# A hybrid decoder block on one core: the sums for the down weights paced two at a time, and a warm-up of fp32r products in seven operand orders

## The chip, the core and the metric

The kernel runs on one core of a Trainium2 chip. The metric is the device time of one execution in microseconds. The profile of one execution, taken on the chip, gives a span from the first to the last instruction.

Five engines work side by side, each through its own queue of instructions in order: TensorE (PE, with its weight loads PEld), VectorE (DVE), ScalarE (ACT), GpSimd (POOL) and SyncE (SP). In this kernel SyncE issues nearly all loads and stores, and GpSimd issues the transfers that add in DRAM.

## The reference

```
h = rms_norm(x, g_mix_pre);  z = h @ w_in                      # x: 512 x 1024
y_pool = pool_mixer(z[:, :512]) @ w_pool_out
y_rnn  = rg_lru_branch(z[:, 512:1536], z[:, 1536:2560]) @ w_rg_out
x = x + rms_norm((gate_pool * y_pool + gate_rnn * y_rnn) @ w_o, g_mix_post)

h = rms_norm(x, g_ffn_pre);  up = h @ w_up                     # 1024 x 6144
hid = gelu(causal_dwconv(up[:, :3072])) * up[:, 3072:]
x = x + rms_norm(hid @ w_down, g_ffn_post)                     # 3072 x 1024

ple = rms_norm(p @ w_ple_proj, g_ple_post)
x = x + sigmoid(rms_norm(x, g_ple_gate) @ w_ple_gate) * ple
```

All inputs are fp32. `w_in` has 4608 columns: 512 for the pooling, 1024 and 1024 for the recurrence, and 2048 for the two gates.

## The kernel before

**Arithmetic.** Every fp32 operand is split into two fp32r parts, a rounded `hi` (a copy on ACT, L193 or L412) and the rest `lo` (a subtraction on VectorE, L189 or L414). A product of two operands is three products of parts, the helper `mm3` (L196 to L200): hi x hi, hi x lo, lo x hi. L198, L199 and L200 therefore stand for nearly all of TensorE's work. The order of TensorE's instructions is the order of the program (`manual_schedule`, L116). The other engines' order is set by a planner from the program order, with priorities (`urgent()`, `high_priority`) and some orders written out by hand (`behind`).

**The opening.** The columns `col` are loaded and `ones` is set (L208). A warm-up follows on TensorE: ten fp32 products of `ones` with itself, 128 columns each (L214 to L216); a product of fp32 shows in the profile as two instructions. Then the transposed input arrives in eight tiles, ACT scales each to `hi` and VectorE makes `lo` (L466, L467), and the first four tiles of the recurrence's input are computed together: 8 chunks x 3 parts x 4 tiles of 512 columns (L497 to L503). Behind them come the remaining tiles of `w_in`, in `in_tile`, with the first L198.

**The middle.** The recurrence, the pooling, their output products and `w_o`. The products with `w_o`, the up weights (for pairs 1 and later) and the down weights use a scheme of seven products for a 2 x 2 block (Strassen's, in the form with sums that follow from each other), so sums of weight blocks are needed: blocks 1, 2, 3 are plain and 5, 7, 6, 4 are sums, numbered by f.

**The up stage.** Pairs p = 0 to 11 of 128-wide column tiles of the gate half and of the linear half. From pair 1 on, `seven(p)` gives the order of a pair's products: f = 1, then 3 of the pair before, then 6, 2, 7, 5, 4. Each f is 24 products of 256 columns (`up_product`, L972). For the block sums of pairs 3 to 11 the four plain blocks are loaded by SyncE (L342, `raw`) and added on VectorE (L348); each is split by L193 and L189. ACT copies or negates results between banks at f = 1 (L985), f = 6 (L990), f = 7 (L992, L993) and f = 5 (L988, into `q5`). The two convolution steps on VectorE are L1000, and the products of `hidden` are L1009 and L1016. Weights are prepared four products ahead (`AHEAD`), six `raw` buffers in turn.

**The sums for the down weights.** `sums_of("wd")` (L253) yields 48 transfers of 512 KB: for each of f = 5, 7, 6, 4 six copies and then six additions in DRAM (`accum_op`) into `wsum`. For 6 and 4 the copies read a sum made before (in the profile `wdsum<-wdsum`); all others read `w_down`. `sum_in_dram` (L269) issues the next n on GpSimd's queue; the first of them waits for an instruction named by `after`, and each follows the one before in the queue. L1088 and L1089 call it once in a pair, after f = 5 from pair 2 on, for six transfers that wait for the copy at L988:

```
if f == 5 and p >= SUMS_FROM:
    sum_in_dram(down_sums, SUMS_EACH, q5_done[0])
```

The last of the 48 go out in pair 9. The down products (`down_product`, L1136) read the sums after the up stage.

**Buffers.** `quad("C")` takes the next of four C buffers, `slot()` the next of 25 m buffers, `bank()` the next of eight PSUM banks. A tile waits until the earlier owner of its buffer is no longer read.

Of the kernel before, what the change touches and what calls it, by code (L numbers as in the profile page):

```python
# [9 lines left out]
F32 = mybir.dt.float32  # L10
F32R = mybir.dt.float32r
AF = mybir.ActivationFunctionType
ALU = mybir.AluOpType

P = 128
S = 512
# [15 lines left out]
HALF = S // 2  # L32
# [14 lines left out]

UP_SUMS = (1, 2)

SUMS_FROM, SUMS_EACH = 2, 6  # L50


PLACES, PLACE_UP, PLACE_H2 = 64, 48, (1072, 46)
URGENT = 700
WARM = 10

FIRST = (0, 256), (256, 512), (512, 1024)
IN_ORDER = [("gate", _g) for _g in range(4)]
# [23 lines left out]
def block_kernel(  # L82
# [21 lines left out]
    ACT, V, PE = nc.scalar, nc.vector, nc.tensor  # L104
# [13 lines left out]
    def urgent():  # L118
        return tc.high_priority(offset=URGENT)
# [3 lines left out]
    def nm(s):  # L123
        uid[0] += 1
        return f"{s}{uid[0]}"

    def bank():
        return psum.tile([P, S], F32, tag="ps", name=nm("ps"))

    def temp(dt=F32, n=S):  # L130
        return tmp.tile([P, n], dt, tag="t", name=nm("t"))

    def slot(dt=F32):
        return mid.tile([P, S], dt, tag="m", name=nm("m"))

    def quad(tag, dt=F32R, place=0):
        t = big.tile([P, 4 * S + PLACES], dt, tag=tag, name=nm(tag))
        return t[:, place : place + 4 * S].rearrange("p (a c) -> p a c", a=4)
# [13 lines left out]
    def behind(ins, name):  # L152
        tc.add_manual_dep(
            ins.ins,
            name,
            mybir.DependencyInfo(mybir.DependencyClass.NoSync, mybir.DependencyReason.DATA),
            reason="order on the engine",
        )
# [24 lines left out]
        last_func[0] = ins.ins.name  # L183
        return ins

    last_copy, h2_done, z_done, q5_done = [None], [None], [None], [None]

    def sub(o, a, b):
        V.tensor_tensor(o, a, b, ALU.subtract)  # L189
# [17 lines left out]
    ones = slot()[:, :P]  # L207
# [4 lines left out]
    ACT.copy(warm, ones[:, 0:1])  # L212

    wps = bank()  # L214
    for _ in range(WARM):
        PE.matmul(wps[:, :P], ones, ones, start=True, stop=True)  # L216

    def c1(j):
        return col[:, j : j + 1]
# [33 lines left out]
    def sums_of(name):  # L253

        if name == "up":
            for p in UP_SUMS:
                for f, start, more in ((5, 11, 12), (7, 12, 22), (6, 5, 22), (4, 6, 21)):
                    yield usum[p, f], usum[p, start] if start < 10 else up_block(p, start), {}
                    yield usum[p, f], up_block(p, more), {"accum_op": ALU.add}
            return  # L260
        for f, start, more in ((5, 1, 0), (7, 0, 3), (6, 5, 3), (4, 6, 2)):
            for q in range(pieces[name]):
                yield wsum[name, f][q], piece_of(name, start, q), {}
            for q in range(pieces[name]):
                yield wsum[name, f][q], block_of(name, more, q), {"accum_op": ALU.add}
# [3 lines left out]
    def sum_in_dram(sums, n, after=None):  # L269

        for o, i, kw in islice(sums, n):
            ins = nc.gpsimd.dma_start(o, i, **kw)
            if after is not None:
                kind = mybir.DependencyClass.Sync, mybir.DependencyReason.DATA
                tc.add_manual_dep(ins.ins, after, mybir.DependencyInfo(*kind), reason="pace of the sums")
                after = None
            if last_sum[0] is not None:
                behind(ins, last_sum[0])
            last_sum[0] = ins.ins.name

    def seven(p):

        return [(p - (f == 3), f) for f in (SEVEN if p > 1 else SEVEN_1) if (f == 3 or p < NPAIR) and (f != 3 or p > 1)]
# [133 lines left out]
    def weight(key, ahead=AHEAD):  # L417
        i = order.index(key)
        while nxt[0] <= min(i + ahead, len(order) - 1):
            prep(order[nxt[0]])  # L420
            nxt[0] += 1
        return ready[key]
# [36 lines left out]
    for k in range(KD):  # L459
# [8 lines left out]
        if k % 2 == 1 and k < 7:  # L468
            if k > 1:
                xt = quad("C", F32)  # L470
                a = k // 2 - 1
# [25 lines left out]
    for k in range(KD):  # L497
        w = weight(("rx", k // 2), ahead=3)
        (wh, wl), (hh, hl) = w, ht(k)
        for i, (a, b) in enumerate(((wh, hh), (wl, hh), (wh, hl))):  # L500
            for m in range(4):
                o = (k % 2) * S + m * P
# [19 lines left out]
    mabs, e, f, s, s2, ncol, n2col = sp  # L522
# [293 lines left out]
    for m in range(KD):  # L816
        w = weight(("wpo", m))
# [3 lines left out]
        w = weight(("wrg", m))  # L821
# [7 lines left out]
        a, b = gate[m], gate[8 + m]  # L829
# [60 lines left out]
    hid, gb, ub = {}, {}, {}  # L890
# [5 lines left out]
    def products(o, w, i, form, start):  # L896
        for k in range(4):
            lhs = tuple(v[:, i, k * P : (k + 1) * P] for v in w)
            rhs = tuple(v[:, k, :] for v in form)
            mm3(o, lhs, rhs, start and k == 0, k == 3, skip_group_check=True)  # L900
# [69 lines left out]
    q5, act_g = {}, {}  # L970

    def up_product(f, p):  # L972
        for i in range(2):
            w = weight(("up", p, f))
            if f == 1 and p > 1:
                gb[i] = bank()
                if p == 2 and i == 0:
                    PE.matmul(gb[i], w[0][:, 0, :P], w[0][:, 0, :], start=True, stop=True)
            o = {1: zb, 6: zb, 7: zb, 2: gb, 4: gb, 3: ub, 5: {0: db, 1: db}}[f][i]
            a = HALF if f == 4 or (f, i) == (5, 1) else 0  # L980
            products(o[:, a : a + HALF], w, i, forms[f], f in (1, 5))
            z = zb[i][:, :HALF]
            with urgent():
                if f == 1 and p > 1:
                    ACT.copy(gb[i][:, :HALF], z)  # L985
                elif (f, i) == (5, 1):
                    q5[p] = temp()
                    q5_done[0] = ACT.copy(q5[p], o).ins.name  # L988
                elif f == 6:
                    ACT.activation(ub[i][:, :HALF], z, AF.Identity, scale=-1.0)  # L990
                elif f == 7:
                    ACT.copy(gb[i][:, HALF:], z)  # L992
                    z_done[0] = ACT.activation(ub[i][:, HALF:], z, AF.Identity, scale=-1.0).ins.name  # L993

    def gated_half(j, pg):
        a = temp()
        with urgent():
            ACT.activation(a, pg, AF.Identity, scale=c1(C_FW + 2 * NJ + j), bias=c1(C_FB + j))
            for d in (1, 2):
                V.scalar_tensor_tensor(  # L1000
                    a[:, d:], pg[:, : S - d], c1(C_FW + (2 - d) * NJ + j), a[:, d:], ALU.mult, ALU.add
                )
        act(a, a, AF.Gelu_apprx_tanh)
        act_g[j] = a

    def hidden(j, pu, q):
        hid[j] = hslot(j)
        if q is not None:
            V.tensor_tensor(  # L1009
                hid[j].rearrange("p (b c) -> p b c", b=2),  # L1010
                pu.rearrange("p (b c) -> p b c", b=2),
                q[:, None, :].to_broadcast([P, 2, HALF]),
                ALU.add,
            )
            pu = hid[j]
        V.tensor_tensor(hid[j], act_g[j], pu, ALU.mult)  # L1016
# [10 lines left out]
    for kind, n in O_AFTER:  # L1027
        if kind == "tr":
            h2_tile(n)
        elif kind == "up":  # L1030
            up_plain(n, 0)
        else:
            up_product(n, 1)
# [48 lines left out]
    down_sums = sums_of("wd")  # L1082
    for p in range(1, NPAIR + 1):
        for q, f in seven(p):
            if (q, f) == (1, 1):
                continue
            up_product(f, q)
            if f == 5 and p >= SUMS_FROM:  # L1088
                sum_in_dram(down_sums, SUMS_EACH, q5_done[0])  # L1089
            if f == 4:  # L1090
                for i in range(2):
                    gated_half(2 * q + i, gb[i])
            if f == 3:
                for i in range(2):
                    hidden(2 * q + i, ub[i], q5[q][:, i * HALF : (i + 1) * HALF])
# [97 lines left out]
    q5 = wpool.tile([P, 2, S], F32, tag="sum", name=nm("sum"), bufs=1)  # L1193
# [38 lines left out]
    for h in range(2):  # L1232
        for t in range(NT):
            i = 2 * (t % 2) + h
            o = temp()
# [3 lines left out]
            for a, b in parts:  # L1239
                ps = bank()  # L1240
                for k in range(KD):
                    if (h, t, k) == (0, 1, 3):
                        x3_tile(2)
                    w = weight(("wpg", k // 2, h))
# [86 lines left out]
```

## Time and profile before

| | us |
|---|---|
| median of 3 runs | 737.29 |
| lowest and highest | 736.93 and 737.32 |
| span of the profiled execution | 735.6 |
| TensorE busy in the span | 728.2 |
| VectorE, ACT, GpSimd busy | 577.8, 443.6, 82.7 |

The profiled execution's own time isn't given beside its span; the runs are 1.7 us longer in the median than the span.

In a timeline row stand start, duration (both in us from the start of the span), engine, line, operation, output<-inputs by the program's names, shape and count; a bracket holds the idle time of the engine before it and what ended it. A "q" behind an engine marks its queue. In the chain of work that ended last, each row is one step: start, us, what. A row of the view by windows holds the window and its length, then for each of PE, PEld, DVE, ACT and POOL the busy time with the number of instructions that touch the window, then the granted TensorE clock, the DMA share and GB/s. TensorE's ends are modelled: products overlap, so the pace is read from starts, and a busy TensorE needn't be at full pace.

### The profile page before, as it was taken

How to read it: one execution, taken by the hardware profiler on the slowest of the kernel's cores; microseconds unless marked ns; L12 is line 12 of the kernel's file. 1: busy time of each engine (PE TensorE's matmuls, PEld its weight loads, DVE VectorE, ACT ScalarE, POOL GpSimd, SP SyncE). 2: the span in 40 equal slices, each digit the busy share in tenths (PEclk: the TensorE clock that was granted, in tenths of full speed). 3: DMA queues.
4: the chain of work that ended last, by engine and by line, in shares of the span. 5: the costliest groups of instructions: out<-in, count | busy, mean ns of one | idle time of the engine just before them, and what ended most of it. 6: DMA issues, size and time to landing. Idle time of an engine off the chain costs nothing.

```text
span 735.6 us, 11212 instructions
## 1 busy us (share of the span) xinstructions
PE 728.2 (99%) x4281; PEld 641.8 (87%) x4281; DVE 577.8 (79%) x749; ACT 443.6 (60%) x670; POOL 82.7 (11%) x107
## 2 busy tenths in 40 slices
PE   9999999999999999999999999999999999999997
PEld 7887778888888888889999999999999888888886
DVE  4896735999646577776989999979799997788852
ACT  6746779844543334477856666666577756565721
POOL 0312112100000000120002323131210000001100
PEclk9999999999999999999999999999999999999999
DMA  8999786664788997895457798979798675768011
GB/s 328 382 309 268 166 238 175 154 198 131 267 297 267 325 327 286 306 333 180 144 191 267 176 321 234 315 206 273 253 246 297 206 250 193 266 201 270 18 58 57
DMA packets 64933, 172.53 MB, mean 235 GB/s; under 512 B 5808, under 2 KB 6448, under 8 KB 64560
## 3 DMA queue, kind: packets, MB, share of 16 engines
q1 hardware_dynamic: 50336, 129.78, 50.9%
q0 software_dynamic: 14400, 41.95, 24.1%
q8 instruction: 33, 0.54, 0.3%
q14 instruction: 20, 0.16, 0.1%
q10 hardware_dynamic: 144, 0.10, 0.0%
HBM read 155.03 MB, written 58.72 MB: 291 GB/s over the span
## 4 chain that ended last, share of the span: by engine, by line
PE 87%; DMA 7%; DVE 3%; issue 1%; ACT 1%; SPq 0%; POOL 0%; DVEq 0%; ACTq 0%
PE ps L198 28%; PE ps L199 28%; PE ps L200 28%; DMA raw<-in_w_up_dram 5%; DMA C<-in_x_dram 1%; DVE lo L189 1%; PE ps L858 1%; DVE raw L348 1%; PE ps L606 1%; DMA m<-in_x_t_dram 1%; PE ps L503 1%; DVE t L1000 1%; ACT C L486 0%; ACT hi L193 0%; SPq L403 0%
## 5 line engine op out<-in xcount | busy, mean ns | idle before, releaser
L189 DVE TENSOR_TENSOR lo<-raw,hi 128x1024 fp32r<-128x1024 f32 (+2 forms) x193 | 224.5, 1183 | 50.1 <-ACT hi L412 29.4
L198 PE MATMUL ps<-A,hi 128*128 128x256 f32 (+1 forms) x608 | 197.8, 325 | 1.1 <-ACT ps L985 1.1
L199 PE MATMUL ps<-A,hi 128*128 128x256 f32 (+1 forms) x608 | 197.1, 324 | 0.0
L200 PE MATMUL ps<-A,lo 128*128 128x256 f32 (+1 forms) x608 | 197.0, 324 | 0.0
L412 ACT CAST hi<-raw 128x1024 fp32r<-128x1024 f32 (+1 forms) x112 | 113.2, 1015 | 108.1 <-PE ps L199 43.2
L198 PEld LDWEIGHTS ps<-A,hi 128*128 128x128 f32 x608 | 114.3, 188 | 12.8 <-ACT ps L985 1.5
L200 PEld LDWEIGHTS ps<-A,lo 128*128 128x128 f32 x608 | 114.1, 188 | 10.1
L199 PEld LDWEIGHTS ps<-A,hi 128*128 128x128 f32 x608 | 114.1, 188 | 9.7
L198 PE MATMUL ps<-C,hi 128*128 128x256 f32 (+1 forms) x392 | 116.9, 298 | 0.0
L200 PE MATMUL ps<-C,lo 128*128 128x256 f32 (+1 forms) x392 | 116.6, 297 | 0.0
L199 PE MATMUL ps<-C,hi 128*128 128x256 f32 (+1 forms) x392 | 116.5, 297 | 0.0
L193 ACT CAST hi<-raw 128x1024 fp32r<-128x1024 f32 x78 | 80.6, 1052 | 33.2 <-PE ps L199 23.3
L198 PE MATMUL ps<-hi,A 128*128 128x512 f32 x224 | 87.4, 390 | 0.0
L200 PE MATMUL ps<-hi,A 128*128 128x512 f32 x224 | 87.2, 389 | 0.0
L199 PE MATMUL ps<-lo,A 128*128 128x512 f32 x224 | 87.1, 389 | 0.0
L198 PEld LDWEIGHTS ps<-C,hi 128*128 128x128 f32 x392 | 73.8, 188 | 2.8 <-ACT rb L441 0.2
L199 PEld LDWEIGHTS ps<-C,hi 128*128 128x128 f32 x392 | 73.8, 188 | 2.6
L200 PEld LDWEIGHTS ps<-C,lo 128*128 128x128 f32 x392 | 73.7, 188 | 2.5
L434 POOL TENSOR_TENSOR s<-s,mhalf 128x1 f32<-128x1 f32 (+1 forms) x21 | 15.8, 754 | 353.9 <-DVE s L447 334.6
L200 PEld LDWEIGHTS ps<-hi,A 128*128 128x128 f32 x224 | 42.0, 188 | 8.8
L199 PEld LDWEIGHTS ps<-lo,A 128*128 128x128 f32 x224 | 42.1, 188 | 8.6
L198 PEld LDWEIGHTS ps<-hi,A 128*128 128x128 f32 x224 | 42.0, 188 | 8.5
(191 smaller groups left out, 1026.2 us busy)
## 6 DMA issues: line engine op xcount, KB each, us to landing
raw<-in_w_up_dram SPq DMA_DIRECT2D x46, 512.0 KB, 7.4
wdsum<-in_w_down_dram POOLq DMA_DIRECT2D x36, 512.0 KB, 13.0
raw<-in_w_in_dram SPq DMA_DIRECT2D x32, 512.0 KB, 6.6
raw<-wdsum SPq DMA_DIRECT2D x24, 512.0 KB, 4.4
raw<-in_w_down_dram SPq DMA_DIRECT2D x18, 512.0 KB, 4.6
wosum<-in_w_o_dram POOLq DMA_DIRECT2D x12, 512.0 KB, 9.8
wdsum<-wdsum POOLq DMA_DIRECT2D x12, 512.0 KB, 12.0
parts<-hi SPq DMA_DIRECT2D x10, 512.0 KB, 3.9
```

The costliest lines, as they stand in the source:

```text
L189: V.tensor_tensor(o, a, b, ALU.subtract)
L193: last_copy[0] = ACT.copy(hi, src)
L198: PE.matmul(o, ah, bh, start=start, stop=False, **kw)
L199: PE.matmul(o, ah, bl, start=False, stop=False, **kw)
L200: PE.matmul(o, al, bh, start=False, stop=stop, **kw)
L348: V.tensor_tensor(o, a, b, ALU.add)
L412: ACT.copy(hi, raw)
L434: last_pow[0] = nc.gpsimd.tensor_tensor(y, v, mhalf[:, :n], ALU.pow).ins.name
L503: PE.matmul(rx[m], a[:, o : o + P], b, start=k == 0 and i == 0, stop=k == KD - 1 and i == 2)
L606: PE.matmul(ps, bd[pr, a, o], b[pr], start=i == 0, stop=i == 2)
L858: PE.transpose(ps[:, q * P : (q + 1) * P], a[:, q * P : (q + 1) * P], ident)
L1000: V.scalar_tensor_tensor(a[:, d:], pg[:, : S - d], c1(C_FW + (2 - d) * NJ + j), a[:, d:], ALU.mult, ALU.add)
```

## The change

The warm-up: VectorE clears 1024 columns of a C buffer, copies 512 of them into two m buffers as fp32r and copies the 1024 onto themselves as fp32r. TensorE then runs 14 products of fp32r with 512 columns, instead of 10 of fp32 with 128: each of seven orders of the moving operand, with both m buffers as the stationary one. The orders are plain; one column repeated; two columns 512 apart in turn; every second column; 16 columns of every 32; plain from column 1; plain from column 8. All values are zero.

The sums: two transfers are issued after each of the products f = 1, 6 and 5 of a pair, from pair 2 on, and wait for ACT's last copy there (L985, L990, L988). That is again six a pair.

```
-SUMS_FROM, SUMS_EACH = 2, 6
+SUMS_FROM, SUMS_AFTER, SUMS_EACH = 2, (1, 6, 5), 2
...
-WARM = 10
...
     wps = bank()
-    for _ in range(WARM):
-        PE.matmul(wps[:, :P], ones, ones, start=True, stop=True)
+    wq = quad("C")
+    V.memset(wq[:, 0:2, :].bitcast(F32), 0.0)
+    wv = wq[:, 0:2, :].rearrange("p a c -> p (a c)")
+    ws = [slot(F32R), slot(F32R)]
+    for w in ws:
+        V.tensor_copy(w, wv[:, :S].bitcast(F32))
+    V.tensor_copy(wv, wv.bitcast(F32))
+    moving = (
+        wv[:, 0:S],
+        wv[:, 0:1].to_broadcast([P, S]),
+        wv.rearrange("p (a b) -> p b a", a=2)[:, 0:HALF, :],
+        wv[:, 0 : 2 * S : 2],
+        wv.rearrange("p (c e) -> p c e", e=32)[:, :, 0:16],
+        wv[:, 1 : S + 1],
+        wv[:, 8 : S + 8],
+    )
+    for m in moving:
+        for i in range(2):
+            PE.matmul(wps, ws[i][:, :P], m, start=True, stop=True)
...
                 if f == 1 and p > 1:
-                    ACT.copy(gb[i][:, :HALF], z)
+                    paced[0] = ACT.copy(gb[i][:, :HALF], z).ins.name
                 elif (f, i) == (5, 1):
                     q5[p] = temp()
-                    q5_done[0] = ACT.copy(q5[p], o).ins.name
+                    paced[0] = ACT.copy(q5[p], o).ins.name
                 elif f == 6:
-                    ACT.activation(ub[i][:, :HALF], z, AF.Identity, scale=-1.0)
+                    paced[0] = ACT.activation(ub[i][:, :HALF], z, AF.Identity, scale=-1.0).ins.name
...
-            if f == 5 and p >= SUMS_FROM:
-                sum_in_dram(down_sums, SUMS_EACH, q5_done[0])
+            if f in SUMS_AFTER and p >= SUMS_FROM:
+                sum_in_dram(down_sums, SUMS_EACH, paced[0])
```

More of the change, by code (lines that the diff above doesn't have):

```diff
@@ L184, in ina @@
         return ins
-    last_copy, h2_done, z_done, q5_done = [None], [None], [None], [None]
+    last_copy, h2_done, z_done, paced = [None], [None], [None], [None]
     def sub(o, a, b):
```

## The prediction

> **What bounds the kernel now.** I read the page first, then TensorE's waits, then the order of time at the two places that the diff touches. The page says that TensorE is busy throughout and that the chain that ended last runs along it.
>
> ```profile
> span 735.6 us, 11212 instructions
> PE 728.2 (99%) x4281; PEld 641.8 (87%) x4281; DVE 577.8 (79%) x749; ACT 443.6 (60%) x670; POOL 82.7 (11%) x107
> ...
> PE 87%; DMA 7%; DVE 3%; issue 1%; ACT 1%; SPq 0%; POOL 0%; DVEq 0%; ACTq 0%
> ```
>
> The waits of TensorE (waiter, releaser: total us, times, longest) are few: its first product, two waits in the opening products, and two on an ACT copy.
>
> ```profile
> PE ps L198 <- ACT ps L985: 1.1, 2, 0.8
> PE ps L216 <- DVE mhalf L210: 1.1, 1, 1.1
> PE ps L503 <- ACT hi L409: 0.3, 1, 0.3
> PE ps L503 <- DVE lo L189: 0.3, 1, 0.3
> ```
>
> So whatever delays TensorE after its opening stays in the end time one for one, and what better-paced transfers can give back is the wait on L985 and its trail. The page gives the span, 735.6 us, and the runs have a median of 737.29; I take the difference, 1.7 us, as what lies around the span, and make the sums on the span.
>
> **Part 1, the warm-up.** TensorE in order of time: start us, us, what, count.
>
> ```profile
> 1.06 4.12 PE L216 MATMUL ps<-m 128*128 128x128 f32 x20 [1.06 <-DVE mhalf L210]
> 5.03 0.73 PE L503 MATMUL ps<-A,hi 128*128 128x512 f32 x2
> ...
> 25.66 1.07 PE L503 MATMUL ps<-A,hi 128*128 128x512 f32 x4
> ...
> 28.38 0.39 PE L198 MATMUL ps<-A,hi 128*128 128x512 f32 x1
> ```
>
> The old warm-up begins at 1.06 and is over when the first real operands come at 5.03. From 25.66 to 28.38 twelve products start, one per 0.2267 us. The code has 96 L503 products (8 x 3 x 4), so without any wait the 97th (L198) starts 96 x 0.2267 = 21.76 after a first product at T; it started at 28.38. Hence there is **slack**: a T up to 6.62 costs nothing, since it only eats the waits, and each later microsecond costs one. A product that comes later than before finds its operands, as ACT and VectorE make them at the old times.
>
> The new T follows from VectorE, which must first clear 1024 columns, copy 512 columns twice and 1024 once.
>
> ```profile
> 0.84 0.17 DVE L208 MEMSET m<- 128x128 f32 x1 [0.84 <-PEq L1318]
> 0.96 0.06 DVE L210 MEMSET mhalf<- 128x4 f32 x1
> 3.96 0.17 DVE L523 SCALAR_TENSOR_TENSOR sp<-col 128x8 f32<-128x8 f32 x1 [2.94 <-DMA col<-in_cols_dram]
> 4.71 0.75 DVE L467 SCALAR_TENSOR_TENSOR A<-m,col,A 128x512 fp32r<-128x512 f32 x1 [0.59 <-ACT A L466]
> ```
> ```profile
> L748 DVE COPY m<-ps 128x512 f32<-128x512 f32 x4 | 2.6, 680 | 0.0
> ```
>
> The two memsets differ by 0.11 us for 124 columns, 0.89 ns each; 1024 take 0.06 + 0.91 = 0.97 us. No row shows a copy from SBUF on VectorE. From above, the pace of the COPY from PSUM gives 0.68 + 0.68 + 1.36 = 2.72; from below, nothing. I take the memset's pace, the nearest row of work that reads nothing from PSUM: 0.5 + 0.5 + 0.97 = 1.97. After the old memsets (1.02) that puts TensorE's start at 1.02 + 0.97 + 1.97 = 3.96 (2.0 to 4.7). VectorE idled there: L523 got its data at 3.96 and L467 started at 4.71, so at the upper end L523 moves by 0.7 and L467 not at all. (The Trainium skill, "VectorE: DVE Perf Modes", section "Walkthrough: the 8-slice pipeline in each mode", says that a one-source fp32 copy inside SBUF moves two elements a cycle; no row here shows it. By it the copies would be some 0.7 us quicker and the sum that much lower.)
>
> TensorE is slow at first. Two stretches of the old warm-up, each the products that touch one instant, and the durations (minimum, median, maximum):
>
> ```profile
> 3.99 0.63 PE L216 MATMUL ps<-m 128*128 128x128 f32 x2
> ```
> ```profile
> 4.68 0.50 PE L216 MATMUL ps<-m 128*128 128x128 f32 x3
> ```
> ```profile
> L216 PE MATMUL ps<-m x20: 275/421/581, 1.1 to 4.9; 128*128 128x128 f32 x20
> ```
>
> At 3.99 two take 0.63, with 0.42 each (the median) one every 0.21; at 4.68 three take 0.50, with 0.275 each one every 0.11. So the pace doubles between 4.2 and 4.7; I take 4.45, 3.4 us after the first product, and the same 3.4 after a first product at 3.96. With 0.453 each (twice 0.2267) that holds 7.5 of the 14 new products; the other 6.5 take 1.47. T = 3.96 + 3.4 + 1.47 = 8.83, and the part costs 8.83 - 6.62 = **+2.2 us**. (The Trainium skill, "TensorE: Matmul & The Clock Gate", section "Part 1: The HAM clock gate (the "warmup" mystery)", has a free-running window of 3.4 us, so that the slow time varies from run to run; the switch in this trace agrees with 3.4 and cannot show the variation. By it up to 6.8 us could be slow, and the cost up to 3.7.)
>
> Bounds: a start at 2.0 gives +0.3, one at 4.7 +3.0; from 3.96, all 14 fast gives 3.96 + 3.17 - 6.62 = +0.5 and all 14 slow +3.7. No row shows a spread moving operand: if the ten products of the last five orders were read at half pace, 10 x 0.2267 = +2.3 came on top; the other way, no row excludes a small gain. I take the pace of every 512-column row.
>
> The buffers that the change takes from the C and m pools stand at the head of their rings, so later tiles move by one and two places and wait for the tile that they waited for before, but for the first lap, whose owners (the warm-up's and `ones`, read last in the opening) are done by then. I count nothing; without that cover an early tile would wait for L548.
>
> **Part 2, the sums.** Today six go out after the copy L988. GpSimd's issues (start, us to issue, count), then the DMA issues of three stretches (KB, median us to landing): without sums, beside six additions, beside six copies of sums.
>
> ```profile
> 409.25 6.36 POOL L272 DMA_DIRECT2D wdsum<-in_w_down_dram  x6 [15.07 <-ACT t L988]
> ...
> 506.08 2.04 POOL L272 DMA_DIRECT2D wdsum<-wdsum  x4 [11.05 <-ACT t L988]
> 511.54 0.49 POOL L272 DMA_DIRECT2D wdsum<-wdsum  x1 [3.41 <-DMA wdsum<-in_w_down_dram]
> ```
> ```profile
> raw<-in_w_up_dram SPq DMA_DIRECT2D x3, 512.0 KB, 3.3
> ```
> ```profile
> raw<-in_w_up_dram SPq DMA_DIRECT2D x4, 512.0 KB, 9.4
> ```
> ```profile
> wdsum<-wdsum POOLq DMA_DIRECT2D x6, 512.0 KB, 12.0
> raw<-in_w_up_dram SPq DMA_DIRECT2D x4, 512.0 KB, 12.6
> ```
>
> The second burst of copies (506) ends in the only wait of this stage. The chain, then TensorE itself, then its products (x) in ten microseconds before and behind the wait:
>
> ```profile
> 508.10 18.25 DMA raw<-in_w_up_dram
> ```
> ```profile
> 530.92 0.28 PE L200 MATMUL ps<-A,lo 128*128 128x256 f32 x1
> 531.47 0.38 PE L198 MATMUL ps<-A,hi 128*128 128x256 f32 x1 [0.28 <-ACT ps L985]
> ```
> ```profile
> 532.83 0.28 PE L200 MATMUL ps<-A,lo 128*128 128x256 f32 x1
> 533.92 0.38 PE L198 MATMUL ps<-A,hi 128*128 128x256 f32 x1 [0.82 <-ACT ps L985]
> ```
> ```profile
> 519.00:529.00 10.00, 10.00 (x89) 10.00 (x89) 5.85 (x6) 4.79 (x9) 0.00 (x0) 1.00 0.76 249
> 534.00:544.00 10.00, 10.00 (x85) 10.00 (x86) 10.00 (x13) 6.02 (x12) 1.53 (x2) 1.00 1.11 237
> ```
>
> A block of the up weights lands 18.25 us after its issue; its copy, its subtraction and the sums with it run late, VectorE falls behind (10.00 of 10.00 busy), and L985 with it. At 10.00 / 89 = 0.112 a product, the gaps of 0.55 and 1.09 lose 0.44 + 0.98 = 1.42 us. Behind the wait TensorE holds 85 products where it held 89: 0.45 at most, counted as 0.4. In all **1.8 us** can come back.
>
> With two at a time a block issued beside copies has two ahead of it. The six land after 12.0 us in the median, with three or four done, some 3 us each; four fewer take up to 12 off 18.25. I take the latency of the nearest row, 9.4 beside additions, where TensorE had no wait. Forecast: the wait goes, -1.8; bounds -1.8 and, if other blocks come late, a wait of the same size more. The sums also begin five products earlier, where the DMA (next to last column its share) has room:
>
> ```profile
> 370.00:390.00 20.00, 20.00 (x171) 19.96 (x170) 16.36 (x19) 12.54 (x21) 0.00 (x0) 1.00 0.46 153
> ```
> ```profile
> 390.00:556.00 166.00, 164.91 (x1436) 164.51 (x1435) 150.39 (x165) 107.54 (x171) 39.55 (x48) 1.00 0.95 262
> ```
>
> The waits that a pair now has (on L985, L990, L988) are GpSimd's, whose queue then holds only other sums, read a stage later by the down products. The count stays 48, with the last two at the old last place. What the first ones meet are blocks issued a pair ahead of use: going from 3.3 to 9.4 us is what later pairs bear already.
>
> **Sum:** 735.6 + 2.2 - 1.8 = 736.0 for the span, 737.7 with what lies around. A measurement of this kernel tells about 0.2%, 1.5 us, from no change.
>
> **Rivals.**
> - *The wait stays.* The DMA share is full whatever the pairs, and a sum that waits for the one that it reads holds GpSimd's queue (3.41 us at 511.54), so that pairs can bunch; then only the warm-up counts, 737.3 + 2.2 = 739.5. For the gain speaks that blocks wait longer beside copies (12.6) than beside additions (9.4), where the wait did not occur. Chance 0.18. (The Trainium skill, "DMA: Bandwidth & Descriptors", section "Queues, rings and completion order", has each DMA engine take turns between queues packet by packet; by that, how many sums stand in GpSimd's queue would not matter to SyncE's blocks. The trace cannot tell, as both bursts are six deep.)
> - *The warm-up is longer* (slower side): TensorE reads the spread orders at half pace. The cost passes the gain from T = 8.4 on, and 1.5 us more from 9.9. With 2.2 + 2.3 - 1.8: 740.0. For it: no such operand in the trace; against: the first of them fall in the slow time. Chance 0.13.
> - *The warm-up hides*: copies that cost next to nothing, cost 0.3 and the wait gone, 737.3 - 1.5 = 735.8. For it: the slack of 6.62; against: the memset alone takes 0.97. Chance 0.14.
> - *The change sets another pace for later products.* The trace has two paces for the same products, 85 and 89 in ten microseconds; as far again on the quick side, 4%, would be some 29 us less, 708. Against: after each wait 0.2267 came back by itself. Chance 0.03.
> - My forecast, 736.3 to 739.0: 0.52.
>
> **Numbers.** The range goes from the hidden warm-up to the longer one with a little room, 735.4 to 740.2, and leaves out less than 2 in 10. Faster by over 0.2% (under 735.8): half of the hidden case, the new pace and a tenth of the forecast's case, 0.15. Slower (over 738.8): both slower rivals and a tenth of the forecast's, 0.36. Within: 0.49.
>
> **What would show it.** Right: the first L503 near 8.8 and no wait before L503, L198 at 30.6, no wait on L985, no up block over about 12 us. Wrong: warm-up products that differ by order at the quick pace; up blocks still near 18 us; waits of TensorE elsewhere between 370 and 560; VectorE's new work elsewhere than at the start, as its order is the planner's.

## The result and the profile after

Measured in turn on one chip, the changed kernel takes 738.69 us in the median (738.04 to 739.51, 12 runs) and the kernel before 736.91 (734.68 to 737.97, 12 runs). The ratio is 1.0026, with a 95% interval of 1.0017 to 1.0034: slower by 1.8 us between the medians and 1.9 by the ratio, just past the 0.2% that can be told from no change. The execution that was profiled is the slowest of the twelve, 739.51 us, so its trace tells somewhat more than the median.

The page of the changed kernel: span, busy times, and the chain that ended last. TensorE was and is the bound.

```profile
span 737.7 us, 11217 instructions
...
PE 728.6 (99%) x4275; PEld 642.4 (87%) x4275; DVE 580.2 (79%) x753; ACT 444.0 (60%) x670; POOL 82.4 (11%) x107
...
PE 99%; DMA 0%; DVE 0%; ACT 0%; issue 0%
```

The span grew by 2.1 us. Lines have moved: L503 is now L519, the three products of parts are L197 to L199, and the copy that TensorE waited for, L985, is L1001. TensorE's waits are down to one row, its own first product:

```profile
PE ps L232 <- DVE C L220: 4.5, 1, 4.5
```

Both waits on L985 are gone, and both in the opening. The copies of sums in the page's list of DMA issues (KB, median us to landing):

```profile
wdsum<-wdsum POOLq DMA_DIRECT2D x12, 512.0 KB, 7.0
```

The copies landed 12.0 us after issue, now 7.0. The slowest block of the up weights between 360 and 560 us, issued at 492.02, is this row; it was 18.25:

```profile
raw<-in_w_up_dram SPq DMA_DIRECT2D x1, 512.0 KB, 14.6
```

The work of the two stretches that the prediction showed, one ahead of the old wait and one behind it, lies in these windows now (PE, PEld, DVE, ACT, POOL busy with counts, clock, DMA share, GB/s):

```profile
523.00:533.00 10.00, 10.00 (x89) 10.00 (x88) 8.40 (x10) 7.91 (x13) 2.09 (x2) 1.00 1.10 241
536.00:546.00 10.00, 10.00 (x91) 10.00 (x90) 8.38 (x9) 5.51 (x11) 0.00 (x0) 1.00 0.73 205
```

TensorE goes from 89 products to 91 where it fell from 89 to 85, and VectorE, which went from 5.85 to a full 10.00, is busy 8.4 in both. So the half with the sums did its work. What was lost lies at the start; TensorE, then VectorE, in order of time:

```profile
4.52 6.27 PE L232 MATMUL ps<-C,m 128*128 128x512 f32 x14 [4.52 <-DVE C L220]
10.63 1.08 PE L519 MATMUL ps<-A,hi 128*128 128x512 f32 x4
```
```profile
32.40 0.39 PE L197 MATMUL ps<-A,hi 128*128 128x512 f32 x1
```
```profile
1.18 0.91 DVE L215 MEMSET C<- 128x1024 f32 x1 [0.16 <-issue]
2.13 0.76 DVE L219 CAST m<-C 128x512 fp32r<-128x512 f32 x2
3.69 0.17 DVE L539 SCALAR_TENSOR_TENSOR sp<-col 128x8 f32<-128x8 f32 x1 [0.80 <-DMA col<-in_cols_dram]
3.78 0.69 DVE L220 CAST C<-C 128x1024 fp32r<-128x1024 f32 x1
```

The warm-up begins at 4.52. Its 14 products take 10.63 - 4.52 = 6.11 us, 0.436 each, so all of them ran at the slow pace (the last begins at 10.27; the pace doubles at 10.54). The first L197 starts at 32.40, where its counterpart L198 started at 28.38: 4.0 us later. The prediction's 1.8 for the sums taken off, 2.2 remain, and the span grew by 2.1.

### The profile page after: what moved, and what is told of

Its sections match the earlier page's. It is cut to its first block, busy times and chain, and to the rows that moved or that the text cites. A ratio compares the mean times of both kernels' runs of the same rounds, so it can differ in the third digit from the quotient of the medians.

```text
span 737.7 us, 11217 instructions
## 1 busy us (share of the span) xinstructions
PE 728.6 (99%) x4275; PEld 642.4 (87%) x4275; DVE 580.2 (79%) x753; ACT 444.0 (60%) x670; POOL 82.4 (11%) x107
## 4 chain that ended last, share of the span: by engine, by line
PE 99%; DMA 0%; DVE 0%; ACT 0%; issue 0%
PE ps L197 31%; PE ps L198 31%; PE ps L199 31%; PE ps L519 3%; PE ps L874 1%; PE ps L622 1%; PE ps L232 1%; DMA col<-in_cols_dram 0%; PE ps L564 0%; DVE C L220 0%; ACT t L163 0%; DVE t L1265 0%; DVE t L1266 0%; PE ps L994 0%; DVE sp L539 0%
## 5 line engine op out<-in xcount | busy, mean ns | idle before, releaser
L197 PE MATMUL ps<-A,hi 128*128 128x256 f32 (+1 forms) x608 | 197.5, 325 | 0.0
L198 PE MATMUL ps<-A,hi 128*128 128x256 f32 (+1 forms) x608 | 197.0, 324 | 0.0
L199 PE MATMUL ps<-A,lo 128*128 128x256 f32 (+1 forms) x608 | 196.9, 324 | 0.0
L197 PEld LDWEIGHTS ps<-A,hi 128*128 128x128 f32 x608 | 114.3, 188 | 11.3 <-issue 1.1
L199 PEld LDWEIGHTS ps<-A,lo 128*128 128x128 f32 x608 | 114.1, 188 | 9.9
L198 PEld LDWEIGHTS ps<-A,hi 128*128 128x128 f32 x608 | 114.1, 188 | 9.9
L197 PE MATMUL ps<-C,hi 128*128 128x256 f32 (+1 forms) x392 | 116.8, 298 | 0.0
L199 PE MATMUL ps<-C,lo 128*128 128x256 f32 (+1 forms) x392 | 116.5, 297 | 0.0
L198 PE MATMUL ps<-C,hi 128*128 128x256 f32 (+1 forms) x392 | 116.5, 297 | 0.0
L197 PE MATMUL ps<-hi,A 128*128 128x512 f32 x224 | 87.5, 390 | 0.0
L199 PE MATMUL ps<-hi,A 128*128 128x512 f32 x224 | 87.2, 389 | 0.0
L198 PE MATMUL ps<-lo,A 128*128 128x512 f32 x224 | 87.1, 389 | 0.0
L197 PEld LDWEIGHTS ps<-C,hi 128*128 128x128 f32 x392 | 73.8, 188 | 2.8 <-ACT rb L457 0.2
L198 PEld LDWEIGHTS ps<-C,hi 128*128 128x128 f32 x392 | 73.8, 188 | 2.5
L199 PEld LDWEIGHTS ps<-C,lo 128*128 128x128 f32 x392 | 73.7, 188 | 2.5
L199 PEld LDWEIGHTS ps<-hi,A 128*128 128x128 f32 x224 | 42.0, 188 | 8.9
L197 PEld LDWEIGHTS ps<-hi,A 128*128 128x128 f32 x224 | 42.0, 188 | 8.6
L198 PEld LDWEIGHTS ps<-lo,A 128*128 128x128 f32 x224 | 42.1, 188 | 8.6
```

What stands on the lines that cost most here:

```text
L197: PE.matmul(o, ah, bh, start=start, stop=False, **kw)
L198: PE.matmul(o, ah, bl, start=False, stop=False, **kw)
L199: PE.matmul(o, al, bh, start=False, stop=stop, **kw)
```

## The experiments

The theory after the first trace: the two parts are independent; the sums give back the wait, some -1.5 us, and the warm-up costs 3 to 4 us, since its 14 products are all slow and start only at 4.5. The rivals: the spread operand orders cost the time; or the new buffers, which shift the order of the opening, do; and for the sums, that their earlier start helped and not their pace. "Before" is each time the kernel before on the same chip.

### The new sums alone

All hunks of the diff but the warm-up's; the ten old products stay.

```
-SUMS_FROM, SUMS_EACH = 2, 6
+SUMS_FROM, SUMS_AFTER, SUMS_EACH = 2, (1, 6, 5), 2
```

> Only the new pace of the sums, with the old warm-up. Theory: the two parts are independent, and the sums alone take away the wait on the copy at f = 1 and its trail: no wait of TensorE between 370 and 560 us, no up block over 13 us to landing, 1.8 us less than before (ratio 0.9976). Rival: the wait went only because the warm-up shifted TensorE against the transfers; then a wait on the copy stays and the ratio is 1.000.

Measured: 735.24 us beside 736.52, ratio 0.9979 (0.9968 to 0.9990). TensorE's waits in its trace:

```profile
PE ps L216 <- DVE mhalf L210: 1.1, 1, 1.1
PE ps L503 <- ACT hi L409: 0.6, 1, 0.6
PE ps L503 <- DVE lo L189: 0.4, 1, 0.4
PE ps L858 <- DVE h L1164: 0.3, 1, 0.3
```

The waits on L985 are gone; the gain of 0.21%, 1.5 us, agrees with the 1.8 of the prediction. This kernel beats both.

### The new warm-up alone

Only the warm-up's hunk; the sums go out six at a time as before.

```
-    for _ in range(WARM):
-        PE.matmul(wps[:, :P], ones, ones, start=True, stop=True)
+    wq = quad("C")
...
+    for m in moving:
+        for i in range(2):
+            PE.matmul(wps, ws[i][:, :P], m, start=True, stop=True)
```

> Only the new warm-up, with the six sums at one place. Theory: the first L503 product starts between 9.4 and 10.7 us, depending on when the pace doubles, the opening costs 2.8 to 4.0 us in the profile, and the wait of about 1.4 us on the copy at f = 1 is still there; ratio 1.004 to 1.005. Rival (the shift removes the wait): ratio 1.002 to 1.003 and no wait between 500 and 540 us.

Measured: 740.34 us, ratio 1.0047 (1.0029 to 1.0065), some +3.5 us. One of its waits is the old one on the copy (L1001 is the old L985). Another, of 1.3 us near the end (L874 for a DVE result), stands neither in the trace of before nor in that of the changed kernel, and what it is worth in the timed runs stays open.

```profile
PE ps L197 <- ACT ps L1001: 0.8, 1, 0.8
```
```profile
4.55 5.90 PE L232 MATMUL ps<-C,m 128*128 128x512 f32 x14 [4.55 <-DVE C L220]
10.29 1.09 PE L519 MATMUL ps<-A,hi 128*128 128x512 f32 x4
```

The wait stays without the new sums, and the opening is late without them: the parts are independent as far as the intervals can tell, and -1.5 and +3.5 make the +1.9 of the whole (0.9979 x 1.0047 = 1.0026).

### Fourteen products, all in the plain order

```
-    moving = (
-        wv[:, 0:S],
...
-    )
+    moving = (wv[:, 0:S],) * 7
```

> The new warm-up with 14 products that all read the moving operand plainly, old sums. Theory: the orders cost nothing at the slow pace, so each product takes 0.427 us as with the orders and the time is that of the new warm-up alone within 0.1%. Rival: the orders are what makes the warm-up long; then products start 0.227 us apart from the first quick one on, the first L503 starts near 8 us, and the ratio is about 0.0015 below that of the new warm-up alone.

Measured: 739.98 us, ratio 1.0042 (1.0028 to 1.0057), the same as with the seven orders within the intervals.

```profile
4.39 5.58 PE L224 MATMUL ps<-C,m 128*128 128x512 f32 x14 [4.39 <-DVE C L220]
9.81 1.08 PE L511 MATMUL ps<-A,hi 128*128 128x512 f32 x4
```

The orders are not what costs. The theory's 0.427 for each product did not hold: the fourteen take 9.81 - 4.39 = 5.42 us, 0.387 each, since the last three already ran at the quick pace (why the switch moves from trace to trace is told below). In the changed kernel the products of every second column start 0.46 and 0.45 us apart and the plain ones 0.427, so even the slowest order adds next to nothing there.

### The seven orders at the quick pace

In the changed kernel no order ran at the quick pace. Here 45 products of the old kind (90 in the trace) stand ahead of the fourteen.

```
+    for _ in range(45):
+        PE.matmul(wps[:, :P], ones, ones, start=True, stop=True)
     wq = quad("C")
```

> Ninety old warm-up products on 128 columns of fp32 ahead of the fourteen with the seven orders, the old sums: the fourteen then run at the quick pace, which in the changed kernel they did not. One look for the pace of each order; the time is not of interest (TensorE's opening is some 7 us longer by intent). Theory: each order 0.227 us a product. Rival (of the prediction): the spread orders at half pace, 0.45 us for those of one repeated column, two interleaved halves, every second column or sixteen of each 32.

Measured in one run: 747.70 us beside 737.34, with an opening that is longer by intent. First all fourteen as one row; then products 6 to 8 and 10 (the sixth is of two interleaved halves, 7 and 8 of every second column, the tenth of sixteen of each 32), each from an instant that it alone touches; then the first real ones:

```profile
13.27 3.91 PE L234 MATMUL ps<-C,m 128*128 128x512 f32 x14
```
```profile
14.47 0.38 PE L234 MATMUL ps<-C,m 128*128 128x512 f32 x1
```
```profile
14.69 0.63 PE L234 MATMUL ps<-C,m 128*128 128x512 f32 x1
```
```profile
15.14 0.65 PE L234 MATMUL ps<-C,m 128*128 128x512 f32 x1
```
```profile
15.86 0.41 PE L234 MATMUL ps<-C,m 128*128 128x512 f32 x1
```
```profile
17.02 1.08 PE L521 MATMUL ps<-A,hi 128*128 128x512 f32 x4
```

From start to start: the first five (plain, one column repeated, interleaved) take (14.47 - 13.27) / 5 = 0.24 each. It is 0.22 for the interleaved halves, 0.45 for the seventh, and (15.86 - 15.14) / 2 = 0.36 over the eighth and ninth. Every second column is thus read at half pace once TensorE is quick. Products 10 to 14 take (17.02 - 15.86) / 5 = 0.23 each. The rival was right of one order of seven and wrong of the rest; the theory was wrong of that one. This run shows the prediction's slack once more: 17.02 + 21.76 = 38.78, and the first L197 started at 38.80.

### Seven products instead of fourteen

```
     for m in moving:
-        for i in range(2):
+        for i in range(1):
```

> One product of each order instead of two (7 in all), old sums. Theory 1, the slow time lasts a given time from the first product whatever runs in it (3.4 to 6.0 us): the first L503 starts at 4.5 + 7 x 0.427 = 7.5, and if the pace doubles only near 10.5 some seven L503 products run slow as well, so that the opening costs 2.4 us; if it doubles by 8, 0.9 us. Ratio 1.001 to 1.003. Rival: the number of warm-up products decides when the pace doubles; then it doubles later than 11 us and the ratio is no lower than with all 14.

Measured: 741.65 us, ratio 1.0064 (1.0045 to 1.0082): slower than with fourteen. The theory had 1.001 to 1.003 and missed. The rival's signs came true, a quick pace later than 11 us and a ratio no lower than with fourteen, but its cause, the number of products, is refuted by the next runs: there seven do bring the quick pace.

```profile
4.62 3.36 PE L232 MATMUL ps<-C,m 128*128 128x512 f32 x7 [4.62 <-DVE C L220]
9.97 2.07 PE L519 MATMUL ps<-A,hi 128*128 128x512 f32 x4 [1.98 <-ACT A L482]
11.84 1.91 PE L519 MATMUL ps<-A,lo 128*128 128x512 f32 x4
13.55 2.33 PE L519 MATMUL ps<-A,hi 128*128 128x512 f32 x8
15.72 0.61 PE L519 MATMUL ps<-A,lo 128*128 128x512 f32 x2
```

Two things went wrong. TensorE idled 1.98 us for the first scaled tile of the input (A, L482), which came at 9.97. And behind the gap it was still slow: (13.55 - 9.97) / 8 = 0.45 each, then (15.72 - 13.55) / 8 = 0.27, so the quick pace came near 14. Why the tile came so late shows in the order of the opening. In the kernel before, SyncE's first load is a tile of the input, and ACT's first work on the operands is to scale it:

```profile
0.75 0.38 SPq L401 DMA_DIRECT2D m<-in_x_t_dram  x1
```
```profile
3.96 0.72 ACT L466 ACTIVATE A<-m,col 128x512 fp32r<-128x512 f32 x1 [1.29 <-DMA col<-in_cols_dram]
```

In the changed kernel, whose opening has the order of this run, ACT and then SyncE's queue:

```profile
8.14 1.04 ACT L428 CAST hi<-raw 128x1024 fp32r<-128x1024 f32 x1 [1.77 <-DMA raw<-in_w_rx_dram]
9.09 2.56 ACT L482 ACTIVATE A<-m,col 128x512 fp32r<-128x512 f32 x4
```
```profile
0.75 1.34 SPq L419 DMA_DIRECT2D raw<-in_w_rx_dram  x3
...
2.60 0.43 SPq L417 DMA_DIRECT2D m<-in_x_t_dram  x1
```

SyncE now issues the weights ahead of the first tile of the input, and ACT splits the weights ahead of scaling the tiles. The prediction took both from the old order. With fourteen products nothing shows of it, since 10.63 is later than 9.8 or so.

### The two copies in the C buffer, fourteen and seven products

That new order might come from the two m buffers that the warm-up takes, as the input's tiles lie in the same pool. So here the copies lie in the two unused planes of the warm-up's own C buffer; the old sums.

```
-    ws = [slot(F32R), slot(F32R)]
+    ws = [wq[:, 2 + i, :] for i in range(2)]
```

> The new warm-up with the two copies in the two unused planes of its own C buffer instead of two buffers of the m pool; the old sums. With that the opening loads and copies stand in the order of the kernel before. Theory (the 14 products at the slow pace set the end of the opening, the order of the loads only a floor below it): VectorE lets TensorE begin near 4.5, 14 x 0.427 = 6.0 us, first real product near 10.5, first x-lo product near 32.3, the time as with the new warm-up alone, 1.0045 of before (1.003 to 1.006). Rival (the m buffers and the new order of the opening cost the time): first real product near 8.8, at most +2.2 us, 1.003 or less, and the wait in the opening shorter.

> The same with seven products, one of each order, and the old sums; the operands of the first real products are there by 5, as in the kernel before, so TensorE does not idle behind the warm-up. Theory (TensorE goes to the quick pace some 4.5 to 6 us after its first product as long as it is kept busy, by whatever products): the warm-up ends at 4.5 + 3.0 = 7.5, real products at the slow pace up to about 10, which loses 1.2 us, first x-lo product near 7.5 + 21.8 + 1.2 = 30.5, some +2 us on before, 1.0027; with the quick pace at 10.5 1.0034. Rival (seven products on few operands do not bring the quick pace, as with the seven that left a gap, where it came at 14.2): 3.3 us lost, first x-lo product near 32.5, 1.0055.

In both the loads of the opening stand in the old order again. Measured: 739.69 us, ratio 1.0039 (1.0026 to 1.0052), with fourteen; 738.48 us, 1.0022 (1.0011 to 1.0032), with seven of them. With fourteen:

```profile
4.76 5.66 PE L232 MATMUL ps<-C 128*128 128x512 f32 x14 [4.76 <-DVE C L220]
10.25 1.09 PE L519 MATMUL ps<-A,hi 128*128 128x512 f32 x4
```

With seven:

```profile
4.76 3.36 PE L231 MATMUL ps<-C 128*128 128x512 f32 x7 [4.76 <-DVE C L220]
7.92 1.13 PE L518 MATMUL ps<-A,hi 128*128 128x512 f32 x4
8.90 1.08 PE L518 MATMUL ps<-A,lo 128*128 128x512 f32 x4
```

With fourteen the order of the opening costs nothing that can be measured (1.0039 beside 1.0047, the intervals overlap). With seven there is no gap behind the warm-up, the four products from 7.92 take (8.90 - 7.92) / 4 = 0.245 each, and the time is 0.4% below that of the seven that left a gap. Seven fewer slow products are worth 1.2 us beside fourteen, though the intervals overlap. With fourteen the theory held: the first L197 came at 32.06. With seven its time held (1.0022 for 1.0027), but not the pace that it counted on: the products are quick from 8 us on and not from 9 to 10.5, and the first L197 came at 29.77 and not at 30.5.

### No warm-up, with the new sums

```
-    wps = bank()
-    for _ in range(WARM):
-        PE.matmul(wps[:, :P], ones, ones, start=True, stop=True)
```

> The new sums and no warm-up products at all. It measures what a warm-up is worth here, and so whether the opening has the slack of the prediction. Theory (up to a first real product near 6.6 nothing is lost but the slow pace; the quick pace comes 3.4 to 5.6 us after the first product): first real product near 5, slow up to 8.5 to 10.5, which loses 1.7 to 2.7 us of products, first x-lo product at 28.5 to 29.5, some 0.2 to 1 us on the new sums alone, 0.998 to 0.9995 of before. Rival (the warm-up carries the opening): the quick pace comes much later without it, first x-lo product at 31 or more, 1.001 or more.

Measured: 736.32 us beside 737.34, ratio 0.9991 (0.9982 to 1.0000).

```profile
5.14 2.08 PE L500 MATMUL ps<-A,hi 128*128 128x512 f32 x4 [5.14 <-ACT hi L406]
7.02 1.84 PE L500 MATMUL ps<-A,lo 128*128 128x512 f32 x4
```
```profile
28.68 0.39 PE L198 MATMUL ps<-A,hi 128*128 128x512 f32 x1
```

As the theory expected. The first eight real products are slow (0.47 and some 0.42), and the opening ends at 28.68, 0.3 us behind the kernel before, and within the 28.34 to 29.32 at which it ends in the five traces with the old warm-up. The old warm-up thus gives about 1 us at most (0.9991 beside 0.9979, overlapping), and the new one costs more than that.

### Six at a time, one pair earlier

The old sums and warm-up, with the first burst in pair 1.

```
-SUMS_FROM, SUMS_EACH = 2, 6
+SUMS_FROM, SUMS_EACH = 1, 6
```

> The kernel before with its sums still six at one product of a pair, but one pair earlier; the old warm-up. It tells the earlier start of the sums from their pace. Theory (six copies in one go are what puts a block of the up weights off): blocks issued beside the copies still land after 12 to 18 us, and a wait on an ACT copy near 530 or in another pair stays, 0.999 to 1.001 of before. Rival (the new sums helped because they begin earlier and leave the busiest stretch): no such wait, 0.998, as with two at a time.

Measured: 741.51 us, ratio 1.0064 (1.0047 to 1.0081). Two of its waits, and the slowest block of the up weights, issued at 493.34:

```profile
PE ps L198 <- ACT ps L990: 3.6, 1, 3.6
...
PE ps L198 <- ACT ps L985: 0.9, 2, 0.5
```
```profile
raw<-in_w_up_dram SPq DMA_DIRECT2D x1, 512.0 KB, 18.2
```

An earlier start at the old pace does not help: the late block comes with its burst (18.2 us, one pair ahead), and the first burst brings a new wait of 3.6, from which the chain leads back over two blocks of the up weights, from 378.08 (7.99 us) and from 366.92 (7.32 us), just beside that burst, where a block with no sums beside it took 3.3 (the prediction's rows). The theory's direction held, its 0.999 to 1.001 did not: what six at once cost seems to depend on the pair that they meet, which this one trace argues and does not show.

### Two at a time, begun as late as before

```
+            if f in SUMS_AFTER and (p, f) >= (SUMS_FROM, 5) and (p, f) != (2, 6):
+                sum_in_dram(down_sums, SUMS_EACH, paced[0])
```

> The sums two at a time at three products of a pair, but none of them earlier than the first six of the kernel before (pair 2, product 5; the last ones therefore later); the old warm-up. Theory (the pace makes the gain): no wait on an ACT copy, 0.998 of before, as with the sums alone. Rival (the earlier start makes it): the wait stays, 1.000.

Measured: 735.08 us beside 736.70, ratio 0.9977 (0.9967 to 0.9986), with no wait on an ACT copy; the up block that is issued at 506.98, near the one that had taken 18.25, takes:

```profile
raw<-in_w_up_dram SPq DMA_DIRECT2D x1, 512.0 KB, 12.0
```

The whole gain is there without the earlier start: it is the pace.

### Three at a time

```
+SUMS_FROM, SUMS_AFTER, SUMS_EACH = 2, (1, 5), 3
```

> The sums three at a time at two products of a pair (behind products 1 and 5), from the same pair on; the old warm-up. Between six and two. Theory (what delays a block of the up weights is the number of copies that stand beside it, and only a delay past what the wait needs costs): the copies of sums land after some 8 to 9 us (12.0 at six, 7 at two), no block over about 14 us, no wait on an ACT copy, 0.998 of before as with two at a time. Rival (two is the point from which it goes well): a wait on an ACT copy of some 0.5 us or more stays, 0.999 to 1.000.

Measured: 735.77 us beside 737.34, ratio 0.9978 (0.9970 to 0.9987). The copies land after 8.7 us in the median; the slowest up block, issued at 411.45:

```profile
raw<-in_w_up_dram SPq DMA_DIRECT2D x1, 512.0 KB, 10.5
```

The same gain as with two. Two is no threshold; somewhere between three and six the block comes too late.

## Why the prediction was right or wrong

**The time is in the range, and the sum is some 1.5 us too low against before.** The prediction had +0.4 us, the runs show some +1.9. It gave "within 0.2%" the best chance, 0.49, and the ratio is 1.0026. The direction was right and the place in the range is partly luck, since the term for the warm-up was too small.

**What bounds the kernel, and the slack: right.** That each later microsecond of the first real product costs one from 6.62 on gives 10.63 + 21.76 = 32.39 for the first L197, and it started at 32.40. The run with the orders at the quick pace gave 38.78 and 38.80. No wait on L519 was left, as foretold. The 6.62 itself is one draw: with the same opening code the first L198 came at 28.34 to 29.32 in five traces (28.38 before, 28.84 with the new sums alone), which puts the slack at 6.6 to 7.6.

**The sums: right.** -1.8 was forecast; the runs gave -1.5 to -1.7 with the new pace, started early or late, in twos or threes. The block no longer lands at 18 us, VectorE is no longer full there, and TensorE keeps its 89 to 91 products in ten microseconds. The rival that the wait stays is refuted, and so is the thought beside it that the number of sums in GpSimd's queue would not matter to SyncE's blocks: the slowest up block took 18.25 with six at a time, 10.5 with three and 12.0 to 14.6 with two. A block over 12 us did occur (14.6), and cost nothing. Lateness as such does not cost: in the kernel before, a block beside the first burst of copies was nearly as late as that of 18.25, and TensorE did not wait behind it.

```profile
468.77 17.10 DMA raw<-in_w_up_dram
```

**VectorE's start: 0.56 of the error.** 4.52 was measured, 3.96 forecast. The copies were quicker than the memset's pace that I had chosen: 0.76 for both of 512 columns and 0.69 for 1024, 1.45 in place of 1.97. (The rule of two elements a cycle from the Trainium skill, "VectorE: DVE Perf Modes", section "Walkthrough: the 8-slice pipeline in each mode", by which the prediction's estimate had them some 0.7 us quicker, goes the right way; the copies were 0.5 quicker.) (The trace of before did hold copies inside SBUF on VectorE, L752 for one, but of one column, 0.15 us each; no pace can be read from them.) But L539 (before, L523), which waits for `col`, stood ahead of the last copy and held it for 0.80 us, which hid that error and turned it round. The prediction's last sentence had named the planner's order as what might make it wrong, and gave it no price.

**The slow pace: 1.24 of the error, and the step that failed.** "3.4 us after the first product, and the same 3.4 after a first product at 3.96" was read from one trace. In the changed kernel the warm-up took 6.11 us in place of 4.87; all fourteen products were slow in place of 7.5. The step that failed is to take the slow time as fixed from the first product on. Together the two terms make the 1.8 by which T came out at 10.63 and not 8.83, the term at +4.0 and not +2.2. The Trainium skill, "TensorE: Matmul & The Clock Gate", section "Part 1: The HAM clock gate (the "warmup" mystery)", has the window run free; by the prediction's estimate from its 3.4 us, up to 6.8 us can then be slow. By that the prediction gave a cost up to 3.7, and with the start at 4.52 its case of all fourteen slow gives 4.52 + 14 x 0.436 - 6.62 = 4.0. The traces side with the rule against my single row: from the first product to the quick pace it was 3.4 us in the trace of before, 3.2 with seven products and no gap, and 6.0 in the changed kernel. One opening, unchanged, shows it too. With the new sums begun late TensorE's first rows were

```profile
1.06 4.64 PE L216 MATMUL ps<-m 128*128 128x128 f32 x20 [1.06 <-DVE mhalf L210]
5.35 1.76 PE L503 MATMUL ps<-A,hi 128*128 128x512 f32 x4
6.96 1.08 PE L503 MATMUL ps<-A,lo 128*128 128x512 f32 x4
```

and its twenty instructions take (5.35 - 1.06) / 20 = 0.21 each to their end, where before the pace had doubled by 4.7; here it does so only among the four products from 5.35 on (0.40 on the average).

The record of the granted clock tells why. Each trace keeps it as a list of stretches with start, length and share. The first stretch at 1.00 begins where the products double their pace; ahead of it nothing is listed, which the views print as 1.00 too. Eight of the thirteen traces (us):

| trace | first product | clock 1.00 from | time between | length of that stretch / 3.4133 |
|---|---|---|---|---|
| before | 1.06 | 4.49 | 3.43 | 214 |
| three at a time | 1.06 | 4.01 | 2.95 | 214 |
| two at a time, begun late | 1.06 | 6.01 | 4.95 | 213 |
| changed | 4.52 | 10.54 | 6.02 | 213 |
| new warm-up alone | 4.55 | 9.76 | 5.21 | 214 |
| fourteen in the plain order | 4.39 | 8.94 | 4.55 | 213 |
| seven, with the gap | 4.62 | 14.24 | 9.62 | 213 |
| seven, no gap | 4.76 | 7.99 | 3.23 | 213 |

The last column is a whole number in all thirteen (with the early burst 112, then one stretch at 0.50, then 102), so the clock switches on a grid of 3.413 us. Counting back along it, TensorE was busy for at least 2.95 of the 3.41 us ahead of the first switch in every trace, and for at most 2.79 in each earlier stretch. So the slow time depends on where the first product falls in the grid and on gaps: it was 2.95 to 6.02 us in the twelve traces without a gap behind the warm-up, 4.4 on the average, and the prediction's 3.4 is one of the short draws. No run set the place in the grid at will; it came by chance in each.

The profile of the changed kernel is also a late one. With fourteen products the first L197 came at 32.40 here and at 32.10 with the new warm-up alone, and the timed cost of the fourteen products is +2.9 to +3.5 us in three kernels. So over the runs the error of this term is nearer to 1 us than to 1.8. With -1.5 in place of -1.8 for the sums that makes 1.3 of the 1.5 us; the rest is within the intervals.

**"A product that comes later than before finds its operands": false as a rule.** ACT and VectorE did not make them at the old times; the two m buffers moved the loads and the scaling, and the first product had a floor near 9.8. The fourteen slow products covered that; seven did not (1.0064 beside 1.0022). The prediction counted the shifted buffers at nothing and looked only at who last read them, not at what a shift does to the order.

**The slower rival: right in its direction, wrong in its mechanism.** It gave 740.0 for spread orders at half pace, 1.3 us over the measured 738.69 (the forecast's 737.7 is 1.0 under it). Fourteen products in the plain order cost the same, so the orders are not the cause. The mechanism does exist, for every second column alone, and at the quick pace (at the slow pace 0.45 to 0.46 beside 0.43).

## What to carry to other kernels

A warm-up ahead of a loaded engine has a budget, here a first real product at 6.6 to 7.6 us, since the later waits would have eaten that time, and every product past it is paid in full; price it with all its products slow, since a single trace shows one draw of how long that lasts, and leave no gap behind it. Bulk transfers in DRAM that nobody waits for should go out in small groups along the stage, since a burst of them delays the one transfer that somebody does wait for. And a changed buffer or helper tile in an opening can reorder other engines' queues: compare the order before the times.

## What the runs showed of the hardware

- A moving operand of every second column ran at 0.45 us a product of 512 columns at the quick pace, a plain one at 0.227. One of two interleaved halves ran at 0.22. At the slow pace every second column took 0.45 to 0.46 beside 0.427.
- The granted clock switched on a grid of 3.413 us in all thirteen traces, 2.95 to 6.02 us after the first product where no gap came between.
- A pause of 2.0 us in TensorE's first work went with a much later quick pace: at 14.24, 9.62 us after the first product and 4.3 us after the pause. The stretch of the grid from 4.00 had 2.79 us of work, the one from 7.41, with the pause, 1.44, and the one from 10.83 was full. That is one trace.
- A long pause inside the kernel cost twice. Behind the 3.6 us wait of the run with the early burst the granted clock fell, two stretches of the same grid:

```profile
385.53:388.95 3.42, 1.44 (x12) 1.44 (x13) 1.73 (x2) 1.86 (x4) 0.00 (x0) 1.00 0.07 25
388.95:392.36 3.41, 3.41 (x19) 3.41 (x18) 2.04 (x3) 2.54 (x4) 0.00 (x0) 0.50 0.47 154
```

TensorE, busy for 1.44 us of the first, had half the clock for the whole of the second: 19 products, where the next 3.41 us hold 30. The stretch ahead of these two, with 1.82 us of work, was followed by no drop, and behind the 0.82 us wait of the kernel before the clock stayed at 1.00 (the row from 534 in the prediction).
